# Six weight tiles instead of four in the group behind each norm of the feed-forward stages

## The chip, the cores and the metric

The kernel runs on one core of a Trainium2 chip. The metric is the device time of one execution in microseconds. TensorE (PE) multiplies, PEld is its weight load, VectorE (DVE), ScalarE (ACT) and GpSimd (POOL) work elementwise, SyncE (SP) issues most loads. SBUF is the on-chip memory, PSUM the eight banks that TensorE writes to.

## The reference

Two transformer blocks follow each other on one sequence of 256 tokens and 2048 channels, in float32. Each has mixers and feed-forward stages behind RMS norms. The change touches the three feed-forward stages:

```python
# first block, one stage
f = jnp.square(jax.nn.relu(rms_norm(h, norm_mlp_pre[i]) @ mlp_w1[i])) @ mlp_w2[i]
h = h + rms_norm(f, norm_mlp_post[i])
# second block, two stages (layer 0 and 1)
gate, up = jnp.split(rms_norm_2(h, g[2]) @ w_ffn_in, 2, axis=-1)
h = h + rms_norm_2((jax.nn.silu(gate) * up) @ w_ffn_out, g[3])
```

The first has 8192 hidden channels, the other two 5632 each. The output is h after both blocks.

## The kernel before

**Numbers.** Float32 values are multiplied as two float32r parts, high and low. `split` (L243) makes them of an activation tile, `wload` (L255) of weights: a load into `wr`, the high part `wh` on ScalarE (L263), the low part `wl` on VectorE (L264). The pool has four buffers for each of `wr`, `wh` and `wl`, so the split of a chunk needs the buffer of the chunk four before it.

**A group.** `group` (L289) multiplies several weight tiles of 128 output channels, j, with all 16 tiles x of 128 input channels, k. Each j has a PSUM bank of its own. The weights come in chunks of `kc` = 2 k's and four j's, 1024 columns. For each k and j there are two products (L306): `wh` with both parts of x, 512 columns, and `wl` with the high part, 256 columns. Afterwards `evac` (L365) adds the halves of a bank (ScalarE L382, VectorE L384), and the stage's own operations make the hidden tile H of it.

**The banks.** There are eight: four of the tag "ps", two "px", two "pm" (L193). With `self.alt` set, as it is in the feed-forward stages, a group takes four "ps" banks, or two "px" and two "ps", or two "ps" and two "px" in turn (L301 to L303, counted by `gpar`, which `post_norm` sets so that the first group of a stage takes four "ps"). Small matters and the background work take "pm".

**The first group of a stage** stands right behind the norm before it, and its x does not exist yet. `pre(k)` (L546) makes it: `upd` (L599) adds the normed output to h (VectorE L603), `tile_T` (L585) turns a tile of h by two transposes on TensorE (L591) into half a "px" bank, so two k's share a bank; then ScalarE makes the high part of x (L250) and VectorE the low part (L251). The second transposes of a bank wait until the first half has been read. The norm's factor (L551) is worked out beside that and is multiplied in later.

**The order.** Each engine runs its own queue of instructions in order. The queues are filled ahead of time by a scheduler that takes what is ready by its model, in the order of priorities. Background work for the S5 mixer (`bg_step`) has a lower priority and runs mainly on GpSimd.

**The stages.** `mlp` (L1157) and `ffn` (L1546) go through the hidden channels in four or three parts. A part has groups of four tiles (in `ffn` two tiles of the gate and the same two of the up half), then the product with the second weight (`outs`, L349, `atok`, L334).

Of the kernel before, what the change touches and what calls it, by code (L numbers as in the profile page):

```python
# [18 lines left out]
P = 128  # L19
# [118 lines left out]
class K:  # L138
# [150 lines left out]
    def group(self, Xk, ks, load, ntile=4, pre=None, narrow=None, tag="ps", kc=2):  # L289

        nc = self.nc
        narrow = not self.alt if narrow is None else narrow
        lhs = lambda w, kk, j: w[:, kk, j * P:(j + 1) * P]
        if narrow:
            banks = [self.ps(tag) for _ in range(ntile // 2)]
            ps = [banks[j // 2][:, (j % 2) * T:(j % 2 + 1) * T] for j in range(ntile)]
        else:
            tags = ["ps"] * 4  # L300
            if self.alt:  # L301
                self.gpar = (self.gpar + 1) % 3
                tags = [["ps"] * 4, ["px", "px", "ps", "ps"], ["ps", "ps", "px", "px"]][self.gpar]  # L303
            ps = [self.ps(tags[j]) for j in range(ntile)]
        n = len(ks)
        mm = lambda o, w, x, a, z: nc.tensor.matmul(o, w, x, start=a, stop=z, skip_group_check=True)  # L306
        for c in range(0, n, kc):
            if pre:
                for k in ks[c:c + kc]:
                    pre(k)  # L310
            wh, wl = load(ks[c])

            order = [(kk, j) for j in range(ntile) for kk in range(kc)]
            if pre and c + kc < n:
                order = [(kk, j) for kk in range(kc) for j in range(ntile)]
            if narrow:
                for kk, j in order:
                    i = c + kk  # L320
                    X = Xk(ks[i])
                    mm(ps[j], lhs(wh, kk, j), X[:, 0], i == 0 and j % 2 == 0, False)
                    mm(ps[j], lhs(wh, kk, j), X[:, 1], False, False)
                    mm(ps[j], lhs(wl, kk, j), X[:, 0], False, i == n - 1)
            else:
                for a in range(0, len(order), 2):
                    for kk, j in order[a:a + 2]:
                        mm(ps[j], lhs(wh, kk, j), Xk(ks[c + kk]), c + kk == 0, False)
                    for kk, j in order[a:a + 2]:
                        mm(ps[j][:, 0:T], lhs(wl, kk, j), Xk(ks[c + kk])[:, 0], False, c + kk == n - 1)  # L330
            self.mix_step()
        return ps
# [252 lines left out]
    def tile_T(self, k, bank={}):  # L585

        if k % 2 == 0:
            bank[0] = self.ps("px")
        pt = bank[0][:, (k % 2) * T:(k % 2 + 1) * T]
        for c in range(2):  # L590
            self.nc.tensor.transpose(pt[:, c * P:(c + 1) * P], self.h[:, c, k * P:(k + 1) * P], self.ident)  # L591
        return pt
# [564 lines left out]
    def mlp(self):  # L1157
        nc, I = self.nc, self.I
        V, S = nc.vector, nc.scalar
        X, pre = self.make_x(("mlp_pre", 0))  # L1160
        W1, W2 = I["mlp_w1"], I["mlp_w2"]
        Y = self.newY()
        ss = self.sums()
        ks = list(range(16))
        for ch in range(4):
            H = self.newX()
            self.bg_drain = ch == 3
            for gi in range(4):
                if not pre:
                    self.bg_step(1.5)  # L1170
                c0 = ch * 2048 + gi * 512
                ps = self.group(lambda k: self.xk(X, k), ks, lambda k0: self.wload([((slice(None),), self.wsrc(W1, k0, c0))]),
                                pre=pre)
                if pre:
                    pre = None
                    self.dump("h1", self.h)
                    r2 = self.s([P, 2], tag="r2")
                    rt = self.h_norm()
                    V.tensor_tensor(r2, rt, rt, op=ALU.mult)
                for j in range(4):  # L1180
                    z = self.evac(ps[j])
                    f = self.e()
                    V.scalar_tensor_tensor(f, z, 0.0, z, op0=ALU.max, op1=ALU.mult)
                    behind = self.split(self.xk(H, gi * 4 + j), f)

            def step(gi):
                if ch < 3:
                    self.bg_step(1.5)
                elif gi < 2:
                    self.bg_step(1)  # L1190
                elif gi == 2:
                    self.bg_clean()

            for cols, pv in self.outs(lambda k: self.xk(H, k), ks, W2, ch * 16, ch == 3, step):
                self.add_up(Y, cols, pv, ch, ss if ch == 3 else None, 1)
        self.ple_proj(0, behind)
        self.upd = self.post_norm(Y, ss, r2)
        self.ple_proj(1)
# [347 lines left out]
    def ffn(self, layer):  # L1546
        nc, I = self.nc, self.I
        V, S = nc.vector, nc.scalar
        X, pre = self.make_x(("ng2", layer * 64 + 32))
        rb = self.rtile("a")  # L1550
        W1, W2 = I["w_ffn_in_2"][layer], I["w_ffn_out_2"][layer]
        Y = self.newY()
        ss = self.sums()
        sl = lambda a, b: (slice(None), slice(None), slice(a, b))
        k_lo = 0
        for nk in (16, 16, 12):
            H = self.newX()
            for gi in range(nk // 2):
                if not pre:
                    self.bg_step(2)  # L1560
                c0 = (k_lo + gi * 2) * P
                ps = self.group(lambda k: self.xk(X, k), list(range(16)),
                                lambda k0: self.wload([(sl(0, 256), self.wsrc(W1, k0, c0, 2, 256)),
                                                       (sl(256, 512), self.wsrc(W1, k0, 5632 + c0, 2, 256))]),
                                pre=pre)
                if pre:
                    pre = None
                    self.dump("hm%d" % layer, self.h)
                    rt = self.h_norm(rb, "rf")
                for j in range(2):  # L1570
                    zg = self.evac(ps[j], mul=rb)
                    S.activation(zg, zg, AF.Silu)
                    zu = self.evac(ps[2 + j])
                    f = self.e()
                    V.tensor_tensor(f, zg, zu, op=ALU.mult)  # L1575
                    self.split(self.xk(H, gi * 2 + j), f)
            last = k_lo + nk == 44
            for cols, pv in self.outs(lambda k: self.xk(H, k), list(range(nk)), W2, k_lo, last, lambda gi: self.bg_step(2)):
                self.add_up(Y, cols, pv, k_lo, ss if last else None, 2 + layer * 4 + 3)
            k_lo += nk  # L1580
        self.bg_end()
        self.upd = self.post_norm(Y, ss, rt)
# [491 lines left out]
```

## Time and profile before

| | us |
|---|---|
| median of 3 runs (3555.54 to 3560.48) | 3558.7 |
| the profiled execution | 3564.73 |
| its span | 3563.0 |
| TensorE busy | 3424.4 (96%) |
| VectorE busy | 2186.2 (61%) |
| ScalarE busy | 1729.6 (49%) |
| GpSimd busy | 907.8 (25%) |
| first group, stage one: first transpose at | 432.24 |
| first group, stage two | 1721.64 |
| first group, stage three | 2798.43 |

TensorE is busy nearly always, so the places where it is not are what to look at. A row of a timeline gives the start, the time taken, engine, line and operation, and in brackets how long the engine had been idle and which instruction ended that. Products are pipelined: the time of one row overlaps the start of the next. The profiled execution ran 6.0 us longer than the median of the runs.

### The profile page before, as it was taken

Reading aid. Unit: us, or ns where it says so; the run is one execution under the profiler, and the core shown is the slowest. Engines: PE = TensorE matmul, PEld = TensorE weight load, DVE = VectorE, ACT = ScalarE, POOL = GpSimd, SP = SyncE. Lnnn points to the kernel's source line nnn. Section 1 sums busy time; section 2 is a strip of 40 time slices with the busy share of each in tenths; the row PEclk is TensorE's granted clock in tenths of the full one; section 3 lists DMA queues with packets and bytes.
Section 4 is the critical chain, followed back from the end, with each engine's and each line's share of the span. In section 5 each row is a group of like instructions: output and inputs, shape, how many; then the busy total and the mean of one; then the engine's idle time right before and its main releaser. Section 6 shows DMA issues by size and latency. Waiting matters only on the chain.

```text
span 3563.0 us, 53866 instructions
## 1 busy us (share of the span) xinstructions
PE 3424.4 (96%) x19926; PEld 2922.6 (82%) x19926; DVE 2186.2 (61%) x3331; ACT 1729.6 (49%) x2613; POOL 907.8 (25%) x1374
## 2 busy tenths in 40 slices
PE   8999999999999999999899999999689899999998
PEld 8877788888888788998788888788568788888887
DVE  6687774556555657455765566576755655455555
ACT  5656654644444444446444444344454544444444
POOL 0231022299620003000534754565400000000000
PEclk9999999999999999999999999999889999999999
DMA  8634456667766564565576777778976565665654
GB/s 265 213 117 152 150 171 193 186 219 221 244 207 200 171 182 140 148 188 180 167 215 219 243 227 230 233 233 272 288 240 200 152 189 190 192 189 191 192 188 146
DMA packets 510080, 707.60 MB, mean 199 GB/s; under 512 B 43926, under 2 KB 316087, under 8 KB 509816
## 3 DMA queue, kind: packets, MB, share of 16 engines
q1 hardware_dynamic: 477648, 637.38, 57.3%
q0 software_dynamic: 27456, 63.65, 5.7%
q8 instruction: 156, 2.56, 0.3%
q10 hardware_dynamic: 4712, 3.13, 0.3%
q14 instruction: 108, 0.88, 0.1%
HBM read 662.56 MB, written 37.22 MB: 196 GB/s over the span
## 4 chain that ended last, share of the span: by engine, by line
PE 46%; DVE 2%; DMA 1%; issue 1%; ACT 1%; SPq 0%; ACTq 0%; DVEq 0%
PE ps L306 18%; PE px L306 8%; PE ps L814 6%; PE ps L815 6%; PE ps L816 6%; PE pm L1791 1%; PE px L591 0%; DVE wl L264 0%; DMA wr<-in_w_ffn_in_dram 0%; ACT wh L263 0%; DMA G<-in_gain_dram 0%; PE ps L1911 0%; DMA wr<-in_w_ffn_out_dram 0%; PE pm L1923 0%; PE px L1911 0%
## 5 line engine op out<-in xcount | busy, mean ns | idle before, releaser
L264 DVE TENSOR_TENSOR wl<-wr,wh 128x1024 fp32r<-128x1024 f32 x1126 | 1447.0, 1287 | 1206.8 <-ACT wh L263 1204.2
L263 ACT ACTIVATE wh<-wr 128x1024 fp32r<-128x1024 f32 x1126 | 1190.5, 1059 | 1415.1 <-PE ps L816 571.2
L306 PE MATMUL ps<-x,wh 128*128 128x512 f32 (+1 forms) x4672 | 1224.3, 352 | 33.7 <-DVE x L251 17.0
L814 PE MATMUL ps<-wh,x 128*128 128x512 f32 (+1 forms) x2160 | 819.6, 380 | 2.8 <-ACT x L247 1.6
L815 PE MATMUL ps<-wl,x 128*128 128x512 f32 (+1 forms) x2160 | 813.6, 377 | 1.3 <-DVE wl L264 1.3
L306 PE MATMUL ps<-x,wl 128*128 128x256 f32 x3648 | 813.3, 282 | 1.5 <-DVE wl L264 1.5
L816 PE MATMUL ps<-wh,x 128*128 128x512 f32 (+1 forms) x2160 | 812.7, 377 | 0.0
L306 PEld LDWEIGHTS ps<-x,wl 128*128 128x128 f32 x3648 | 692.9, 191 | 120.8 <-DVE wl L264 3.3
L306 PEld LDWEIGHTS ps<-x,wh 128*128 128x128 f32 x4672 | 731.4, 192 | 50.8 <-DVE x L251 21.8
L814 PEld LDWEIGHTS ps<-wh,x 128*128 128x128 f32 x2160 | 407.5, 189 | 84.1 <-ACT x L247 4.7
L816 PEld LDWEIGHTS ps<-wh,x 128*128 128x128 f32 x2160 | 407.2, 189 | 75.6 <-issue 2.2
L815 PEld LDWEIGHTS ps<-wl,x 128*128 128x128 f32 x2160 | 407.8, 189 | 74.0 <-issue 1.6
L306 PE MATMUL px<-x,wh 128*128 128x512 f32 x1216 | 383.8, 396 | 4.1 <-DVE e L384 4.1
L306 PEld LDWEIGHTS px<-x,wl 128*128 128x128 f32 x1216 | 228.4, 188 | 54.7 <-issue 0.8
L306 PE MATMUL px<-x,wl 128*128 128x256 f32 x1216 | 239.9, 278 | 0.0
L306 PEld LDWEIGHTS px<-x,wh 128*128 128x128 f32 x1216 | 186.4, 189 | 8.0 <-issue 4.5
L1833 POOL TENSOR_TENSOR m<-m,m 128x128 f32<-128x128 f32 x128 | 71.2, 576 | 165.8 <-PE pm L1791 164.4
L247 ACT ACTIVATE x<-e 128x256 fp32r<-128x256 f32 x168 | 67.2, 410 | 85.8 <-DVE e L1575 50.2
L248 DVE TENSOR_TENSOR x<-e,x 128x256 fp32r<-128x256 f32 x168 | 79.2, 482 | 13.7 <-ACT x L247 10.8
L591 PE MATMUL px<-cst,x 128*128 128x128 f32 x224 | 53.4, 339 | 34.2 <-DVE x L603 18.9
L1850 POOL TENSOR_TENSOR m<-m,m 128x256 f32<-128x256 f32 x64 | 61.7, 965 | 80.3 <-DMA m<-in_s5bT_dram 80.2
L1832 POOL TENSOR_TENSOR m<-m,m 128x128 f32<-128x128 f32 x128 | 78.9, 639 | 0.6
(489 smaller groups left out, 2623.0 us busy)
## 6 DMA issues: line engine op xcount, KB each, us to landing
wr<-in_w_ffn_in_dram SPq DMA_DIRECT2D x704, 256.0 KB, 3.1
wr<-in_mlp_w_dram SPq DMA_DIRECT2D x256, 512.0 KB, 4.5
wr<-in_w_ffn_out_dram SPq DMA_DIRECT2D x176, 512.0 KB, 4.8
wr<-in_w_in_dram SPq DMA_DIRECT2D x152, 512.0 KB, 3.9
wr<-in_w_out_dram SPq DMA_DIRECT2D x64, 512.0 KB, 3.8
wr<-in_w_glu_dram SPq DMA_DIRECT2D x128, 256.0 KB, 3.0
wr<-in_ple_gate_dram SPq DMA_DIRECT2D x32, 512.0 KB, 3.9
wr<-in_w_in_dram SPq DMA_DIRECT2D x32, 256.0 KB, 3.2
```

The lines of the kernel that those rows point to most:

```text
L247: a = nc.scalar.activation(dst[:, 0], src, AF.Copy)
L248: b = (eng or nc.vector).tensor_tensor(dst[:, 1], src, dst[:, 0].bitcast(F32), op=ALU.subtract)
L263: nc.scalar.activation(wh, wr, AF.Copy)
L264: nc.vector.tensor_tensor(wl, wr, wh.bitcast(F32), op=ALU.subtract)
L306: mm = lambda o, w, x, a, z: nc.tensor.matmul(o, w, x, start=a, stop=z, skip_group_check=True)
L591: self.nc.tensor.transpose(pt[:, c * P:(c + 1) * P], self.h[:, c, k * P:(k + 1) * P], self.ident)
L814: nc.tensor.matmul(ps, xh, wh, start=first, stop=False, skip_group_check=True)
L815: nc.tensor.matmul(ps, xh, wl, start=False, stop=False, skip_group_check=True)
L816: nc.tensor.matmul(ps, xl, wh, start=False, stop=last, skip_group_check=True)
L1832: G_.tensor_tensor(cx[:, q], u_(0), l_(0), op=ALU.mult)
L1833: G_.tensor_tensor(t1[:, q], u_(1), l_(1), op=ALU.mult)
L1850: G_.tensor_tensor(ob[:, :, ri], v4(gb[0][:, 0]), v4(gb[1][:, ri]), op=ALU.mult)
```

## The change

The first group of each stage gets six tiles, in chunks of one k, 768 columns: in `mlp` six tiles, then 4, 4 and 2; in `ffn` three of the gate and three of the up half, then six groups of two and two, then one and one. The last has chunks of four k's, with rows of 256 columns (1 KB) in `mlp` and 128 (512 bytes) in `ffn`. The six tiles take the four "ps" and both "px" banks, so `tile_T` turns h in "pm" banks wherever `alt` is set. `gpar` no longer moves in the first group, so the group behind it is the one that takes four "ps" banks.

```diff
@@ -297,8 +297,8 @@
-            tags = ["ps"] * 4
-            if self.alt:
+            tags = ["ps"] * 4 + ["px"] * 2
+            if self.alt and ntile < 6:
                 self.gpar = (self.gpar + 1) % 3
@@ -585,7 +585,7 @@
         if k % 2 == 0:
-            bank[0] = self.ps("px")
+            bank[0] = self.ps("pm" if self.alt else "px")
@@ -1165,23 +1165,24 @@
-            for gi in range(4):
+            for t0, nt, kc in ((0, 6, 1), (6, 4, 2), (10, 4, 2), (14, 2, 4)) if pre else [(4 * i, 4, 2) for i in range(4)]:
                 if not pre:
                     self.bg_step(1.5)
-                c0 = ch * 2048 + gi * 512
-                ps = self.group(lambda k: self.xk(X, k), ks, lambda k0: self.wload([((slice(None),), self.wsrc(W1, k0, c0))]),
-                                pre=pre)
+                c0 = ch * 2048 + t0 * P
+                ps = self.group(lambda k: self.xk(X, k), ks, lambda k0: self.wload(
+                    [((slice(None),), self.wsrc(W1, k0, c0, kc, nt * P))], (P, kc, nt * P)), ntile=nt, kc=kc, pre=pre)
...
-                for j in range(4):
+                for j in range(nt):
...
-                    behind = self.split(self.xk(H, gi * 4 + j), f)
+                    behind = self.split(self.xk(H, t0 + j), f)
@@ -1555,25 +1556,28 @@
-            for gi in range(nk // 2):
+            parts = [(2 * i, 2, 2) for i in range(nk // 2)]
+            if pre:
+                parts = [(0, 3, 1)] + [(3 + 2 * i, 2, 2) for i in range(6)] + [(15, 1, 4)]
+            for t0, nt, kc in parts:
                 if not pre:
                     self.bg_step(2)
-                c0 = (k_lo + gi * 2) * P
+                c0, w = (k_lo + t0) * P, nt * P
                 ps = self.group(lambda k: self.xk(X, k), list(range(16)),
-                                lambda k0: self.wload([(sl(0, 256), self.wsrc(W1, k0, c0, 2, 256)),
-                                                       (sl(256, 512), self.wsrc(W1, k0, 5632 + c0, 2, 256))]),
-                                pre=pre)
+                                lambda k0: self.wload([(sl(0, w), self.wsrc(W1, k0, c0, kc, w)),
+                                                       (sl(w, 2 * w), self.wsrc(W1, k0, 5632 + c0, kc, w))], (P, kc, 2 * w)),
+                                ntile=2 * nt, kc=kc, pre=pre)
...
-                for j in range(2):
+                for j in range(nt):
...
-                    zu = self.evac(ps[2 + j])
+                    zu = self.evac(ps[nt + j])
```

**TensorE's queue, first stage, before**, around k 3. `ps_4905` to `ps_4908` are the four tiles, `wh_4955` and `wh_4988` chunks of two k's, `px_4977` the bank of k 4 and k 5, `cst` the identity, `x_4881` h:

```order
L306 MATMUL ps_4908<-x_4899,wl_4956 128x256
L591 MATMUL px_4977<-cst,x_4881 128x128 x2
L306 MATMUL ps_4905<-x_4899,wh_4955 128x512
L306 MATMUL ps_4906<-x_4899,wh_4955 128x512
L306 MATMUL ps_4905<-x_4899,wl_4956 128x256
L306 MATMUL ps_4906<-x_4899,wl_4956 128x256
L306 MATMUL ps_4907<-x_4899,wh_4955 128x512
L306 MATMUL ps_4908<-x_4899,wh_4955 128x512
L306 MATMUL ps_4907<-x_4899,wl_4956 128x256
L306 MATMUL ps_4908<-x_4899,wl_4956 128x256
L591 MATMUL px_4977<-cst,x_4881 128x128 x2
L306 MATMUL ps_4905<-x_4899,wh_4988 128x512
```

The transposes of k 4 stand ahead of the products of k 3, those of k 5 ahead of the products of k 4 (`wh_4988`).

**TensorE's queue, first stage, now**, from the last products of k 3 (`wh_4989`) to the first of k 4 (`wh_5014`). `pm_5007` is the bank of k 4 and k 5, `pm_5054` that of k 6 and k 7:

```order
L306 MATMUL px_4910<-x_4899,wh_4989 128x512
L306 MATMUL px_4909<-x_4899,wl_4990 128x256
L306 MATMUL px_4910<-x_4899,wl_4990 128x256
L591 MATMUL pm_5007<-cst,x_4881 128x128 x2
L591 MATMUL pm_5054<-cst,x_4881 128x128 x2
L306 MATMUL ps_4905<-x_4899,wh_5014 128x512
L306 MATMUL ps_4906<-x_4899,wh_5014 128x512
L306 MATMUL ps_4905<-x_4899,wl_5015 128x256
```

The transposes of k 4 and k 6 now stand behind all products of k 3 and right ahead of those of k 4. Between k 4 and k 5 (`wh_5036`) the queue reads:

```order
L306 MATMUL px_4909<-x_4899,wl_5015 128x256
L306 MATMUL px_4910<-x_4899,wl_5015 128x256
L591 MATMUL pm_5007<-cst,x_4881 128x128 x2
L591 MATMUL pm_5054<-cst,x_4881 128x128 x2
L306 MATMUL ps_4905<-x_4899,wh_5036 128x512
L306 MATMUL ps_4906<-x_4899,wh_5036 128x512
```

The products of k 5, 6 and 7 then follow without transposes, and the pattern returns at k 8 and k 12, in all three stages.

**VectorE's queue, first stage, before.** The low parts of x (L251) come in pairs behind each weight split; `px_5010` is the bank of k 6 and k 7, `px_5043` that of k 8 and k 9:

```order
L264 TENSOR_TENSOR wl_5121<-wr_5118,wh_5120 128x1024
L251 SCALAR_TENSOR_TENSOR x_4899<-px_5010,vec,x_4899 128x256
L251 SCALAR_TENSOR_TENSOR x_4900<-px_5043,vec,x_4900 128x256
L264 TENSOR_TENSOR wl_5154<-wr_5151,wh_5153 128x1024
L251 SCALAR_TENSOR_TENSOR x_4900<-px_5043,vec,x_4900 128x256
L251 SCALAR_TENSOR_TENSOR x_4900<-px_5076,vec,x_4900 128x256
```

**VectorE's queue, first stage, now.** `wl_5084` is the chunk of k 7, `wl_5109` that of k 8:

```order
L264 TENSOR_TENSOR wl_5084<-wr_5081,wh_5083 128x768
L251 SCALAR_TENSOR_TENSOR x_4899<-pm_5007,vec,x_4899 128x256
L251 SCALAR_TENSOR_TENSOR x_4899<-pm_5054,vec,x_4899 128x256
L264 TENSOR_TENSOR wl_5109<-wr_5106,wh_5108 128x768
L251 SCALAR_TENSOR_TENSOR x_4899<-pm_5007,vec,x_4899 128x256
L251 SCALAR_TENSOR_TENSOR x_4899<-pm_5054,vec,x_4899 128x256
L264 TENSOR_TENSOR wl_5131<-wr_5128,wh_5130 128x768
L264 TENSOR_TENSOR wl_5156<-wr_5153,wh_5155 128x768
L264 TENSOR_TENSOR wl_5178<-wr_5175,wh_5177 128x768
L251 SCALAR_TENSOR_TENSOR x_4900<-pm_5101,vec,x_4900 128x256
```

The low part of k 4 stands behind the split of chunk 7, which needs the buffer of chunk 3; that of k 5 behind the split of chunk 8, which needs the buffer of chunk 4. ScalarE's queue has the same order with L263 and L250.

## Rows read from the trace of the kernel before

**Rows 1.** Lines, TensorE, 432–482, 1721–1764, 2798–2832: count | busy, mean ns | idle.

```profile
L306 PE MATMUL ps<-x,wh 128*128 128x512 f32 x84 | 29.2, 429 | 4.7 <-DVE x L251 4.7
...
L306 PE MATMUL ps<-x,wh 128*128 128x512 f32 x60 | 23.4, 479 | 7.6 <-DVE x L251 7.6
...
L306 PE MATMUL ps<-x,wh 128*128 128x512 f32 x60 | 21.0, 434 | 4.4 <-DVE x L251 4.4
```

**Rows 2.** Timeline of TensorE, first stage: start, us, operation, count, idle before it.

```profile
432.24 1.67 PE L591 MATMUL px<-cst,x 128*128 128x128 f32 x4 [4.87 <-DVE x L603]
...
434.56 1.20 PE L306 MATMUL ps<-x,wh 128*128 128x512 f32 x2
...
437.27 0.90 PE L306 MATMUL ps<-x,wh 128*128 128x512 f32 x2
...
459.04 0.73 PE L306 MATMUL ps<-x,wh 128*128 128x512 f32 x2 [0.76 <-DVE x L251]
...
463.32 0.73 PE L306 MATMUL ps<-x,wh 128*128 128x512 f32 x2 [0.76 <-DVE x L251]
```

**Rows 3.** Timeline of ScalarE, first stage; L247 is a pass of 256 columns.

```profile
456.27 1.06 ACT L263 ACTIVATE wh<-wr 128x1024 fp32r<-128x1024 f32 x1 [1.72 <-PE ps L306]
...
460.55 1.06 ACT L263 ACTIVATE wh<-wr 128x1024 fp32r<-128x1024 f32 x1 [1.76 <-PE ps L306]
...
474.78 0.40 ACT L247 ACTIVATE x<-e 128x256 fp32r<-128x256 f32 x1
```

**Rows 4.** Timeline of VectorE, first stage; L248 is a pass of 256 columns.

```profile
433.69 0.48 DVE L251 SCALAR_TENSOR_TENSOR x<-px,vec,x 128x256 fp32r<-128x256 f32 x1
...
457.37 1.22 DVE L264 TENSOR_TENSOR wl<-wr,wh 128x1024 fp32r<-128x1024 f32 x1 [2.27 <-ACT wh L263]
458.51 0.87 DVE L251 SCALAR_TENSOR_TENSOR x<-px,vec,x 128x256 fp32r<-128x256 f32 x2
...
476.05 0.42 DVE L248 TENSOR_TENSOR x<-e,x 128x256 fp32r<-128x256 f32 x1
```

**Rows 5.** Windows: length; busy (PE, PEld, DVE, ACT, POOL); PEclk, DMA, GB/s.

```profile
463.50:500.00 36.50, 36.50 (x208) 31.63 (x209) 29.11 (x73) 20.82 (x33) 0.00 (x0) 1.00 0.59 176
1722.00:1760.00 38.00, 30.18 (x154) 24.87 (x153) 28.49 (x52) 17.76 (x37) 27.07 (x45) 0.83 0.43 137
...
2775.00:2790.00 15.00, 15.00 (x128) 15.00 (x127) 7.11 (x9) 6.92 (x12) 0.00 (x0) 1.00 0.70 201
```

**Rows 6.** The chain that ended last, in order of time: start, us, what.

```profile
1839.62 1.39 PE px L306 x8
```

**Rows 7.** Lines, VectorE, 1731 to 1762 in stage two.

```profile
L264 DVE TENSOR_TENSOR wl<-wr,wh 128x1024 fp32r<-128x1024 f32 x5 | 10.7, 2147 | 6.0 <-ACT wh L263 6.0
L251 DVE SCALAR_TENSOR_TENSOR x<-px,vec,x 128x256 fp32r<-128x256 f32 x12 | 5.3, 474 | 1.4 <-ACT x L250 1.4
```

**Rows 8.** Timeline of TensorE, stage two.

```profile
1721.64 1.61 PE L591 MATMUL px<-cst,x 128*128 128x128 f32 x4 [4.92 <-issue]
...
1737.65 0.73 PE L306 MATMUL ps<-x,wh 128*128 128x512 f32 x2 [2.71 <-DVE x L251]
...
1738.53 1.06 PE L306 MATMUL ps<-x,wh 128*128 128x512 f32 x2
...
1760.09 0.73 PE L306 MATMUL ps<-x,wh 128*128 128x512 f32 x2 [1.27 <-DVE x L251]
...
1790.46 0.73 PE L306 MATMUL px<-x,wh 128*128 128x512 f32 x2 [1.83 <-DVE e L384]
...
1794.44 0.70 PE L306 MATMUL px<-x,wh 128*128 128x512 f32 x2 [1.85 <-DVE e L384]
...
1818.78 0.69 PE L306 MATMUL ps<-x,wh 128*128 128x512 f32 x2 [1.79 <-DVE e L384]
...
1820.66 1.05 PE L306 MATMUL ps<-x,wh 128*128 128x512 f32 x2
```

More of the change, by code (lines that the diff above doesn't have):

```diff
@@ L1569, in ffn @@
                     rt = self.h_norm(rb, "rf")
-                for j in range(2):
+                for j in range(nt):
                     zg = self.evac(ps[j], mul=rb)
                     S.activation(zg, zg, AF.Silu)
-                    zu = self.evac(ps[2 + j])
+                    zu = self.evac(ps[nt + j])
                     f = self.e()
                     V.tensor_tensor(f, zg, zu, op=ALU.mult)
-                    self.split(self.xk(H, gi * 2 + j), f)
+                    self.split(self.xk(H, t0 + j), f)
             last = k_lo + nk == 44
```

## The prediction

> **What bounds the kernel now.** I read the lines view of TensorE first, over the first group of each feed-forward stage: the stretch in which x is made tile by tile (transposes, L591; its high half on ScalarE, L250; its low half on VectorE, L251) while TensorE already multiplies. TensorE sits idle there for 4.7, 7.6 and 4.4 us, all of it ended by L251 [rows 1]: 16.7 us is all that filling this idle time can give. The timelines of the first stage show why it waits [rows 2 to 4]. The weights of a chunk are split four chunks ahead, since the tags wr, wh and wl have four buffers; so the split of wh starts when a chunk's last product is done (ScalarE at 456.27), wl follows at 457.37, and L251 stands behind wl in VectorE's queue (458.51). TensorE goes on at 459.04, 2.77 us after the chunk ended; in that time it has only one other k to do, and 0.76 us stay idle. From 463.32 on nothing is idle: TensorE is busy for 36.50 of 36.50 us [rows 5]. So whatever lengthens this first group lengthens the kernel.
>
> **The sum of what is moved.** TensorE's products stay the same in number. I call one weight tile times one k a step: 4 of them take 1.39 us [rows 6], 0.348 us each. What the diff does not say is where the transposes land, and the order tells it. Before, the transposes of k stand at least one k of products ahead of those that use them. After, they stand four at a time: k 4 and 6 behind the products of k 3, and right ahead of those of k 4; then k 5 and 7 behind the products of k 4. So nothing covers the way from transpose to product, seven times in a stage (k 0 to 1, 3 to 4, 4 to 5, 7 to 8, 8 to 9, 11 to 12, 12 to 13). And L250 and L251 stand behind the split of the chunk four ahead, which waits for the very products that have just ended.
>
> *The price of one such gap.* It is the chain of before, 2.77 us, with 768 columns in place of 1024: on ScalarE 1.06 against 0.40 us for 256 [rows 3], so 0.22 less; on VectorE 1.22 against 0.42 [rows 4], so 0.27 less: 2.28 us. Its bounds: 2.77 if a narrow split is no shorter, 2.19 if it shrinks by the full quarter; I take 2.28, as both slopes are measured. Four transposes run inside it.
>
> *A stage, from the first transpose at 432.24.* The products of k 0 start when its L251 is done (433.69 plus 0.53, the same step as 458.51 to 459.04), at 434.22. Four steps there take 2.71 us (434.56 to 437.27), at the lower clock level, so six take some 4.0: 438.2. A gap: 440.5. k 1 to 3: four steps from first product to the split that waits for them are 1.51 us (459.04 to 460.55), six 2.21, each further k 6 x 0.348 = 2.09, so 6.39: 446.9. Then three times gap, k, gap, three k: 2.28 + 2.21 + 2.28 + 6.39 = 13.16. That ends at 486.4, and 0.5 later since the split in the last gap is 1024 wide again: 486.9. Before, 13 x 4 = 52 steps are done at 463.32; the 44 that make 96 follow without idle time, 15.3 us and 0.3 for transposes: 478.9. The difference is **8.0 us**: the idle 4.7 us goes, and seven uncovered gaps come.
>
> *The end of the group.* The next group now takes the four "ps" banks, where it took two free "px" banks. Its first product needs L384 of the first tile, which stands behind a 1024-wide split that waits for k 14: 1.10 + 1.14 for the split, then 0.42 for a pass of 256 columns [rows 4] and 0.05 to be seen, 2.7 us after k 14, while k 15 covers 2.09. That adds **0.6 us**; between nothing (L384 early enough) and 1.5 (one more wl ahead of it).
>
> *Stages one and three:* 8.6 us each; the third has nearly the same idle time as the first [rows 1]. *Stage two:* GpSimd works in it for 27 of 38 us [rows 5], wl takes 2.15 us in the mean instead of 1.22, L251 stays at 0.47 [rows 7], and from first transpose to the products of k 13 it takes 38.45 us (1721.64 to 1760.09 [rows 8]) against 31.08 in the first: 7.4 more. After, some five of the seven gaps fall under GpSimd's work, each longer by three quarters of 0.92, 3.5 us; and two gaps are so long that the clock falls, as it did before after 2.71 us of idle time, 1.3 us each (four steps 2.71 in place of 1.39 us). That makes 6.1 in place of 7.4, so the stage adds 7.3. GPSIMD Engine Reference of the Trainium skill, section 1, says that GpSimd shares its SBUF interfaces with VectorE and collides with instructions of two SBUF inputs: wl is one, L251, with one input in PSUM, is not, and the trace agrees in the two means. If every VectorE instruction were stretched alike, L251's 0.47 would grow too, some 0.4 us a gap and 2 us in all.
>
> *The clock in stages one and three.* A gap has some 1.7 us of idle time beside 0.6 us of transposes. In the trace, 1.79 us idle ahead of 1818.78 were followed by pairs of 1.05 in place of 0.63 us from 1820.66 on, the level of 1.2 GHz; 1.83 and 1.85 us ahead of 1790.46 and 1794.44 were not [rows 8]. So it is a toss of a coin, from none to most of the seven gaps; I take one stretch a stage, 2 x 1.3 = 2.6 us.
>
> *Edits taken at nothing.* Turning h in "pm" leaves the order in the other stages that use it (the gate after the first stage, the S5 mixer, the end) as it was. Four more splits a stage run on ScalarE and VectorE beside products. The last group has weight rows of 512 bytes; the w_glu stage reads such rows at 201 GB/s with TensorE busy for 15.00 of 15.00 us [rows 5]; if that cover failed, a chunk would wait for the part of a load beyond its 2.8 us of products. In stage two, idle time of 1.83, 1.85 and 1.79 us behind late evacuations [rows 8] may shrink as the group before it gets longer: between 0 and -5.5; I take 0, since loads run only four chunks ahead in both.
>
> Sum: 8.6 + 7.3 + 8.6 + 2.6 = **27 us**. On the profiled execution's own 3564.73 us this is 3591.8; it lies 6.0 above the median of the runs, so against 3558.7 it is **3586 us**.
>
> **Rivals.** *The gaps are shorter* (if x did not stand behind the splits, only transpose, L250 and L251 would be on the way: 0.4 + 0.47 + 0.53, 1.4 us): seven gaps lose 0.9 each, a stage is slower by some 2.3, in all +7: 3566. Against it speaks the order on both engines, and that the same queueing sets the 2.77 us now. *The other side, faster:* the idle time is filled as the six tiles suggest. Place: the products of k 4, 8 and 12; price: -4.7, -7.6 and -4.4, less the 0.6 at each end, 3544. It turns on whether the transposes for the next four k run before TensorE is out of ready work; for it speaks that six tiles are 2.09 us a k against a chain of 2.28, so that one k of lead would hide it; against it, that they stand behind all ready products in TensorE's own queue. *The clock:* each gap, not one a stage, leaves a stretch at 1.2 GHz: some five more in stages one and three, three in stage two, 13 x 1.3 = +17: 3603. TensorE: Matmul & The Clock Gate of the Trainium skill, section "A second HAM failure mode: psum-queue depth-cycling", tells of a kernel in which short idle times between groups of products made the clock swing. In the rows it follows one idle time of that length in three [rows 8].
>
> **How the numbers follow.** Chances: forecast 0.76, with its own range from 3575 (no lower clock in stages one and three, the late evacuations gone) to 3598 (four more stretches, the larger bound of the gap); clock 0.10; shorter gaps 0.08; faster 0.06. The range that leaves no more than 2 in 10 out: 3567 to 3600, since it loses most of the clock rival, the faster one and half of the shorter gaps. A measurement of this kernel tells 0.2%, some 7 us, from no change: faster is the one rival, 0.06; same is most of the shorter gaps, 0.06; slower is the rest, 0.88.
>
> **What would show it.** Right: in the first group of a stage TensorE idle seven times for 1.5 to 2 us, ended by L251, each right behind four transposes (or two pairs), idle time of some 12 us a stage in place of 4.4 to 7.6; from first transpose to the end of k 15 some 54 to 55 us in stages one and three; splits of 768 columns at 0.85 us on ScalarE and 0.96 on VectorE; pairs at the lower clock level here and there. Wrong: products of k 4 that follow those of k 3 without idle time, or transposes that the chip has run earlier than the queue says. The sum is mis-sized if the gap is not 2.28, if the 0.6 at the group's end is several us, or if the granted clock of the stages falls far below 0.9.

## The result, and the profile after

The changed kernel takes 3588.2 us (median of 4 runs, 3580.4 to 3589.2) against 3558.9: 1.008 times as long, 95% interval 1.0066 to 1.0094, which is 23 to 33 us. Run again beside later experiments it took 3585.9 against 3560.0, a ratio of 1.0073 (1.0060 to 1.0087). TensorE does the same work in a longer span, as the head of the page shows (busy us, share of the span, instructions):

```profile
span 3578.6 us, 53976 instructions
PE 3425.3 (96%) x19926; PEld 2923.0 (82%) x19926; DVE 2181.5 (61%) x3343; ACT 1728.2 (48%) x2625; POOL 908.9 (25%) x1374
```

The lines of TensorE over the three norm groups, up to the end of k 15, answer [rows 1] (count | busy, mean ns | idle time and what ended it):

```profile
L306 PE MATMUL ps<-x,wh 128*128 128x512 f32 x64 | 21.8, 424 | 12.4 <-DVE x L251 12.4
...
L306 PE MATMUL ps<-x,wh 128*128 128x512 f32 x64 | 22.8, 439 | 15.7 <-DVE x L251 15.7
...
L306 PE MATMUL ps<-x,wh 128*128 128x512 f32 x64 | 22.8, 440 | 11.9 <-DVE x L251 11.9
```

Idle time ended by L251 was 4.7, 7.6 and 4.4 us; it is now 12.4, 15.7 and 11.9, 23.3 us more. The timeline of TensorE in stage one shows it gap by gap, where [rows 2] stood before:

```profile
430.59 1.61 PE L591 MATMUL pm<-cst,x 128*128 128x128 f32 x4 [4.43 <-issue]
...
444.78 0.40 PE L306 MATMUL px<-x,wl 128*128 128x256 f32 x2
445.02 0.60 PE L591 MATMUL pm<-cst,x 128*128 128x128 f32 x4
447.26 0.72 PE L306 MATMUL ps<-x,wh 128*128 128x512 f32 x2 [1.65 <-DVE x L251]
...
449.46 0.60 PE L591 MATMUL pm<-cst,x 128*128 128x128 f32 x4
451.76 0.73 PE L306 MATMUL ps<-x,wh 128*128 128x512 f32 x2 [1.70 <-DVE x L251]
...
478.51 0.73 PE L306 MATMUL ps<-x,wh 128*128 128x512 f32 x2 [2.13 <-DVE x L251]
...
484.66 0.39 PE L306 MATMUL px<-x,wl 128*128 128x256 f32 x2
485.52 0.72 PE L306 MATMUL ps<-x,wh 128*128 128x512 f32 x2 [0.47 <-DVE e L384]
```

The products of k 3 run into the transposes at 445.02; those of k 4 start at 447.26. Four transposes take 0.60 us of these 2.24; the rest is idle. There are seven such gaps, ahead of k 1, 4, 5, 8, 9, 12 and 13; between them nothing is idle. The first is 2.17 us, the next five 2.24 to 2.30. The last one is longer, 2.73 us, as the split in it is 1024 columns wide. ScalarE and then VectorE inside the gap that begins at 445.02, where [rows 3, 4] stood:

```profile
444.98 0.84 ACT L263 ACTIVATE wh<-wr 128x768 fp32r<-128x768 f32 x1 [1.24 <-PE px L306]
445.73 0.82 ACT L250 ACTIVATE x<-pm,vec 128x256 fp32r<-128x256 f32 x2
```

```profile
445.86 0.96 DVE L264 TENSOR_TENSOR wl<-wr,wh 128x768 fp32r<-128x768 f32 x1 [0.20 <-ACT wh L263]
446.73 0.87 DVE L251 SCALAR_TENSOR_TENSOR x<-pm,vec,x 128x256 fp32r<-128x256 f32 x2
```

The split of chunk 7 starts when the products of k 3 are done (444.98), and L250 and L251 follow it on their engines. The transposes were done at 445.62; x waits for a split that TensorE needs only three k's later.

### The profile page after: what moved, and what is told of

The parts are those of the page before. It is cut to its first block, busy times and chain, and to the rows that moved or that the text cites. A ratio compares the mean times of both kernels' runs of the same rounds, so it can differ in the third digit from the quotient of the medians.

```text
span 3578.6 us, 53976 instructions
## 1 busy us (share of the span) xinstructions
PE 3425.3 (96%) x19926; PEld 2923.0 (82%) x19926; DVE 2181.5 (61%) x3343; ACT 1728.2 (48%) x2625; POOL 908.9 (25%) x1374
## 5 line engine op out<-in xcount | busy, mean ns | idle before, releaser
L264 DVE TENSOR_TENSOR wl<-wr,wh 128x1024 fp32r<-128x1024 f32 (+1 forms) x1138 | 1445.0, 1272 | 1233.5 <-ACT wh L263 1225.6
L263 ACT ACTIVATE wh<-wr 128x1024 fp32r<-128x1024 f32 (+1 forms) x1138 | 1192.9, 1050 | 1468.9 <-PE ps L816 559.8
L306 PE MATMUL ps<-x,wh 128*128 128x512 f32 (+1 forms) x4608 | 1202.5, 350 | 53.6 <-DVE x L251 40.3
L814 PE MATMUL ps<-wh,x 128*128 128x512 f32 (+1 forms) x2160 | 818.4, 379 | 3.1 <-ACT x L247 1.6
L306 PE MATMUL ps<-x,wl 128*128 128x256 f32 x3584 | 801.3, 282 | 1.3 <-DVE wl L264 1.3
L306 PEld LDWEIGHTS ps<-x,wh 128*128 128x128 f32 x4608 | 718.8, 192 | 74.9 <-DVE x L251 46.8
L306 PEld LDWEIGHTS ps<-x,wl 128*128 128x128 f32 x3584 | 680.3, 191 | 118.7 <-issue 4.1
L814 PEld LDWEIGHTS ps<-wh,x 128*128 128x128 f32 x2160 | 407.0, 189 | 82.4 <-ACT x L247 4.7
L306 PE MATMUL px<-x,wh 128*128 128x512 f32 x1280 | 404.8, 398 | 0.0
L306 PEld LDWEIGHTS px<-x,wl 128*128 128x128 f32 x1280 | 242.2, 189 | 57.4
L306 PE MATMUL px<-x,wl 128*128 128x256 f32 x1280 | 252.9, 279 | 0.0
L247 ACT ACTIVATE x<-e 128x256 fp32r<-128x256 f32 x168 | 67.2, 409 | 72.5 <-DVE e L1579 35.5
L248 DVE TENSOR_TENSOR x<-e,x 128x256 fp32r<-128x256 f32 x168 | 78.4, 477 | 12.8 <-ACT x L247 9.5
L568 ACT ACTIVATE m<-x 128x512 f32<-128x512 f32 (+2 forms) x116 | 63.2, 547 | 23.4 <-DVE x L1208 11.5
```

The costliest lines, as they stand in the source:

```text
L247: a = nc.scalar.activation(dst[:, 0], src, AF.Copy)
L248: b = (eng or nc.vector).tensor_tensor(dst[:, 1], src, dst[:, 0].bitcast(F32), op=ALU.subtract)
L263: nc.scalar.activation(wh, wr, AF.Copy)
L264: nc.vector.tensor_tensor(wl, wr, wh.bitcast(F32), op=ALU.subtract)
L568: self.last_act = self.nc.scalar.activation(self.m([P, 512])[:, 0:y.shape[-1]], y, AF.Square, accum_out=ss[0][:, c, ss[1]:ss[1] + 1])
L814: nc.tensor.matmul(ps, xh, wh, start=first, stop=False, skip_group_check=True)
```

## The experiments

Beside medians I compare the **first part** of a stage: from its first transpose to the first product with the second weight (L814), as in these rows of TensorE's timeline in stage two, which belong in turn to the kernel before (its transposes began at 1721.64 [rows 8]), the same kernel in a second trace, and the changed kernel:

```profile
1931.33 0.40 PE L814 MATMUL ps<-wh,x 128*128 128x512 f32 x1
```

```profile
1720.57 1.62 PE L591 MATMUL px<-cst,x 128*128 128x128 f32 x4 [4.92 <-issue]
...
1921.31 0.40 PE L814 MATMUL ps<-wh,x 128*128 128x512 f32 x1
```

```profile
1725.81 0.68 PE L591 MATMUL pm<-cst,x 128*128 128x128 f32 x2 [4.43 <-issue]
...
1937.34 0.40 PE L814 MATMUL ps<-wh,x 128*128 128x512 f32 x1
```

| kernel | first part, us, stage 1 / 2 / 3 | median us | ratio to before (95%) |
|---|---|---|---|
| before, trace of the prediction | 103.0 / 209.7 / 191.6 | 3558.9 | |
| before, again (e8) | 102.5 / 200.7 / 191.5 | 3558.8 | 0.9999 (0.9990 to 1.0008) |
| changed | 111.0 / 211.5 / 201.5 | 3588.2 | 1.0080 (1.0066 to 1.0094) |
| changed, again (e5) | 111.0 / 213.4 / 201.4 | 3585.9 | 1.0073 (1.0060 to 1.0087) |
| pm banks alone (e1) | 102.2 / 200.2 / 190.3 | 3556.5 | 0.9994 (0.9985 to 1.0003) |
| four tiles, one k (e2) | 110.2 / 228.9 / 197.9 | 3591.9 | 1.0099 (1.0085 to 1.0113) |
| four tiles, one k, pm (e7) | 107.5 / 209.9 / 195.6 | 3573.2 | 1.0037 (1.0025 to 1.0049) |
| six tiles, two k's ahead (e3) | 97.6 / 203.5 / 186.7 | 3548.7 | 0.9974 (0.9965 to 0.9983) |
| six tiles, one k ahead (e4) | 98.2 / 205.3 / 186.5 | 3545.8 | 0.9968 (0.9957 to 0.9979) |
| four tiles, four k's ahead, pm (e6) | 96.6 / 197.0 / 186.6 | 3543.6 | 0.9952 (0.9939 to 0.9965) |

Each ratio is to the kernel before in runs beside it, whose medians were 3558.4 us for e1 to e4, 3560.0 for e5 to e7 and 3559.2 for e8.

**Theory:** chunks of one k bring the transposes right ahead of the products that use them, and x queues behind a split that waits for the products just done; so seven gaps a stage. **Rivals:** the six tiles, the banks or the group's end cost the time; the lower clock does.

### e1: the pm banks alone

```diff
-            bank[0] = self.ps("px")
+            bank[0] = self.ps("pm" if self.alt else "px")
```

> The kernel before with one edit: h is turned in pm banks in the feed-forward stages; groups stay at four tiles and chunks of two k's. Theory (the loss comes from the seven uncovered gaps): stages one and three as before, within 1 us each, L251-ended idle of 4.7 and 4.4 us stays. In stage two the background products on pm now stand behind the norm group, so the three late evacuations of 1.83, 1.85 and 1.79 us may go: 3553 to 3559 in all. Rival (the banks cost the time): 3565 or more, with new idle time ahead of transposes.

Measured: no difference (0.9994). The banks cost nothing that shows; stage three's first part is 1.2 us shorter than in e8, a little more than the 1 us expected. Stage two took 200.2 us against 209.7 in the trace of the prediction, without the three late evacuations, which looked like a gain of the banks; e8 shows that it is none.

### e2 and e7: four tiles in chunks of one k

In the kernel before, with `px` banks (e2) and with the edit of e1 as well (e7):

```diff
-                c0 = ch * 2048 + gi * 512
-                ps = self.group(lambda k: self.xk(X, k), ks, lambda k0: self.wload([((slice(None),), self.wsrc(W1, k0, c0))]),
-                                pre=pre)
+                c0, kc = ch * 2048 + gi * 512, 1 if pre else 2
+                ps = self.group(lambda k: self.xk(X, k), ks, lambda k0: self.wload([((slice(None),), self.wsrc(W1, k0, c0, kc))], (P, kc, 512)),
+                                kc=kc, pre=pre)
```

and alike in `ffn`.

> The kernel before with chunks of one k, 512 columns, in the first group of each stage; four tiles and px banks stay. Theory (the chunk of one k takes the transposes' lead away): the same seven gaps, each 1.80 us, since the split ahead of x shrinks with its columns (0.44 us less on ScalarE, 0.53 on VectorE than 2.77); norm group of stage one 39.4 us from first transpose to the end of k 15 against 35.6 before, about +3.8 a stage, 3568 to 3572 with one stretch at the lower clock. If the gap is only transposes, L250 and L251 it is 1.4 and the sum +1 a stage, 3562. If it does not depend on columns it is 2.28 and the sum 3580. Rival (six tiles or the banks cost the time): 3559, no new idle time.

The gaps are there, without six tiles or other banks, and have the forecast size. TensorE, ScalarE and VectorE in e2:

```profile
453.35 0.60 PE L591 MATMUL px<-cst,x 128*128 128x128 f32 x4
455.17 0.73 PE L306 MATMUL ps<-x,wh 128*128 128x512 f32 x2 [1.22 <-DVE x L251]
```

```profile
453.36 0.63 ACT L263 ACTIVATE wh<-wr 128x512 fp32r<-128x512 f32 x1 [0.76 <-PE ps L306]
453.90 0.82 ACT L250 ACTIVATE x<-px,vec 128x256 fp32r<-128x256 f32 x2
```

```profile
454.02 0.69 DVE L264 TENSOR_TENSOR wl<-wr,wh 128x512 fp32r<-128x512 f32 x1 [0.70 <-ACT wh L263]
454.63 0.87 DVE L251 SCALAR_TENSOR_TENSOR x<-px,vec,x 128x256 fp32r<-128x256 f32 x2
```

The gap is 1.82 us (453.35 to 455.17; 1.80 was expected, 1.40 without the queue, 2.28 if columns did not matter). So the split ahead of x sets it: 2.24 us behind 768 columns, 1.82 behind 512. But the sum was 20 us too low. In stage one k 15 ends 43.2 us after the first transpose where 39.4 was expected: the last gap is 2.73 us, as the split in it is 1024 columns wide, and products at the lower clock level stand behind the first gap and the last. Most of the 20 us is one wait in stage two that no theory had:

```profile
1760.17 0.60 PE L591 MATMUL px<-cst,x 128*128 128x128 f32 x4
1777.22 0.64 PE L1791 MATMUL pm<-m,m 128*32 128x128 f32 x2 [16.45 <-POOL m L1834]
```

A product of the background work stands in TensorE's queue ahead of the next k, and GpSimd made its operand late; TensorE was idle for 16.45 us.

> Four tiles in chunks of one k, as before, now with h turned in pm banks, so that the background product of stage two, which kept TensorE waiting for GpSimd for 16.45 us, stands far behind the norm group. Theory: that wait goes, the seven gaps of 1.8 us a stage stay: +7 in stage one, +6 in stage three, about -2 in stage two, 3565 to 3573. If it stays at 3590, the wait was not what made the run with px banks slow.

With the product behind the norm group the wait is gone and the time 18.7 us lower. The first parts are longer than in e8 by 5.0, 9.1 and 4.1 us. The median, 3573.2, lies at the upper end of what was expected: the -2 of stage two rested on the trace of the prediction, and e8 shows that to be no usual one.

### e3 and e4: six tiles, with the lead restored

The changed kernel with `pre` called m k's ahead of the products, m = 2 (e3) or 1 (e4):

```diff
-                for k in ks[c:c + kc]:
+                m = 2 if kc == 1 else 0
+                for k in ks[c + m if c else 0:c + kc + m]:
                     pre(k)
```

> The changed kernel, but the transposes and splits of x are written two k's ahead of the products. Theory: the low part of k stands behind the split that waits for the products of k-3, so two k's of products (4.2 us) cover a chain of 2.28; idle time ended by L251 under 1.5 us in stages one and three, and some 2 us in stage two; 3538 to 3548, faster than before. Rival (banks, the narrow last group or the boundary behind the norm group cost the time): 3560 or more although the gaps are gone.

> As the run with two k's ahead, but one k ahead. Theory: the low part of k stands behind the split that waits for the products of k-2, and one k of products, 2.09 us, covers all but 0.2 us of a chain of 2.28: some 13 idle times of 0.2 us a stage, 2 to 3 us; 3546 to 3556. If the chain were longer than 2.28, every tenth of it would add 1.3 us a stage.

Both are faster than before, by 0.26% and 0.32%, with the banks, the narrow last group and the order at the group's end of the change. e4's rows over the norm groups of stages one and three:

```profile
L591 PE MATMUL pm<-cst,x 128*128 128x128 f32 x32 | 7.5, 314 | 5.1 <-issue 4.4 <-DVE x L251 0.6
...
L591 PE MATMUL pm<-cst,x 128*128 128x128 f32 x32 | 7.5, 316 | 6.1 <-DVE x L603 5.7 <-DVE x L251 0.3
```

L251 ends 0.6 and 0.3 us of idle time where it ended 12.4 and 11.9. The 13 times 0.2 us expected of e4 are not there: between the products of two k's stand two transposes as well, about 0.3 us, and 2.09 and 0.3 cover 2.24. That two k's ahead are not better than one was a miss. e3 lies 0.7 us above its range, e4 just below its own. What is left is in stage two. Of the 2 us of idle time ended by L251 that were expected there in e3 5.0 are left, and in e4 5.6 us ahead of transposes and 3.8 ahead of products:

```profile
L306 PE MATMUL ps<-x,wh 128*128 128x512 f32 x90 | 32.2, 444 | 3.8 <-DVE x L251 3.8
...
L591 PE MATMUL pm<-cst,x 128*128 128x128 f32 x32 | 7.6, 315 | 10.2 <-DVE x L251 5.6 <-issue 4.4 <-DVE x L603 0.2
```

### e6: the lead alone

The kernel before with the edit of e1, four tiles and chunks of two k's, and `pre` four k's ahead:

```diff
-                for k in ks[c:c + kc]:
+                m = 4 if kc == 2 and not narrow else 0
+                for k in ks[c + m if c else 0:c + kc + m]:
                     pre(k)
```

> The kernel before with h turned in pm banks and the transposes and splits of x written four k's ahead; four tiles and chunks of two k's stay. Theory (the lead alone matters, not the number of tiles): L251-ended idle time of 4.7 and 4.4 us in stages one and three goes to under 1, stage two loses most of its 7.6 and the three late evacuations of 5.5: 3540 to 3550, as fast as six tiles with the lead. Rival (six tiles fill the idle time, lead alone doesn't): 3553 to 3559, as the run with pm banks alone.

Measured: 3543.6 us, 16 less than before and the fastest here. Its rows over the three norm groups:

```profile
L306 PE MATMUL ps<-x,wh 128*128 128x512 f32 x88 | 29.8, 417 | 0.0
...
L306 PE MATMUL ps<-x,wh 128*128 128x512 f32 x92 | 32.3, 430 | 0.0
...
L591 PE MATMUL pm<-cst,x 128*128 128x128 f32 x32 | 8.4, 349 | 7.5 <-issue 4.9 <-DVE x L251 2.6
...
L306 PE MATMUL ps<-x,wh 128*128 128x512 f32 x88 | 29.8, 416 | 0.0
```

No product waits for L251 any more, and in stage two transposes still do, for 2.6 us. The idle time that six tiles were to fill is filled by four, once x is made early enough. Against e8 the first parts are shorter by 5.9, 3.7 and 4.9 us, 14.5 in all.

### e5 and e8: both kernels once more

No edit.

> The changed kernel once more, on the chip of the runs beside it, for more executions and a second trace. Theory: the three norm groups again have seven gaps each; the median stays within 3582 to 3590 against 3558. In the first trace the three stages explain +17 us against the trace of before, while the medians differ by 29; if this trace lies near 3588, the stretches that are longer than in the first trace show where the other 8 us are (more stretches at the lower clock level behind gaps, or places outside the three stages).

The seven gaps are there in all three stages, and the three first parts agree with the first trace within 1.9 us. The span is 3584.1 us here, and stage two as a whole, up to the first transpose of stage three, took 6.8 us more than in the first trace, about half of it around one late evacuation, which the first trace does not have:

```profile
2386.55 0.70 PE L306 MATMUL ps<-x,wh 128*128 128x512 f32 x2 [2.07 <-DVE e L384]
```

> The kernel before once more, for a second trace. In the first one (3564.73 us, 6 above the median) the first part of stage two took 209.7 us from the first transpose to the first product with the second weight, with three late evacuations of 1.8 us. The traces of the changed kernel lie 18 and 24 us above it, the medians 26 and 29. Theory: the first trace of before holds some 5 us that a usual execution doesn't, in stage two ahead of 1820 or before the first stage: this one shows 204 to 207 there, or an earlier first transpose, with stages one and three at 103 and 191.6 again. Rival: the same times in all places, and the traces of the changed kernel were both quicker than usual.

Stages one and three repeat within 0.6 us; stage two is 9.0 us shorter, since the three late evacuations of [rows 8] do not occur. TensorE works without a pause in the stretch in which they stood (the columns are those of [rows 5]):

```profile
1773.00:1850.00 77.00, 77.00 (x442) 66.88 (x441) 51.14 (x62) 37.99 (x55) 41.72 (x58) 1.00 0.77 233
```

So the trace on which the prediction rests held an incident of 9 us in stage two that another execution of the same kernel does not have. Against e8 the first parts of the changed kernel are longer by 8.5, 10.8 and 10.0 us, 29.3 in all; the medians differ by 29.2 and, beside e5, 25.9. That 29.3 and 29.2 agree is in part chance: the two traces as a whole differ by 22.8 us (3578.6 and 3555.8), since outside the first parts the changed kernel's is 6.5 us shorter, and it is 7.8 us below the median of its runs. With e5's trace it is 31.1 us in the first parts and 28.3 in all.

## Why the prediction was right

**The forecast** was 3586 us; 3588.2 and 3585.9 were measured, inside its own range of 3575 to 3598.

- *The order.* Seven uncovered gaps a stage, each right behind four transposes, as the queue says. No products of k 4 follow those of k 3 without idle time.
- *The price of a gap*, 2.28 us from 2.77 and the two slopes: measured 2.17 to 2.30 us, and 2.73 for the last (2.78 in the sum). The splits took 0.84 and 0.96 us, as the slopes gave, and the slopes hold at 512 columns as well (e2): 0.63 and 0.69, a gap of 1.82.
- *A stage*, 8.0 us by the end of the norm group: in stage one k 15 ends 54.5 us after the first transpose, 54.7 in the sum. The group's end: 0.47 us idle for L384 (485.52), 0.6 in the sum.
- *Stage two*, 7.3 us: the norm group takes 60.2 us to the end of k 15. Before, by the sum's own reckoning (52 steps until the products of k 13, then 44 of 0.348 and 0.3), it took 54.1 in the first trace and 52.7 in e8, so it adds 6.1 to 7.5, where 6.7 was forecast. The whole first part grew by 10.8 us against e8, more than that. 0.87 us of it is seen: the products of the norm's factor (L424) and two of the background now stand behind k 15 (1786.01 to 1786.88), on a TensorE without idle time, and no longer in the norm group; the other 2.4 us is the background's too. Thirty more of its products stand farther behind, in two stretches that begin with these rows:

```profile
1854.03 0.42 PE L1795 MATMUL pm<-m,m 128*32 128x128 f32 x6
...
1901.30 0.42 PE L1795 MATMUL pm<-m,m 128*32 128x128 f32 x8
```

  Each takes 3.2 us (to 1857.20 and to 1904.48) and holds two steps of the stage's own products, 0.7 us. In e8 there is one such stretch, and the other 16 products stand in the norm group, 12 of them right ahead of an idle time of 2.79 us:

```profile
1745.66 0.63 PE L1791 MATMUL pm<-m,m 128*32 128x128 f32 x12
...
1874.13 0.43 PE L1791 MATMUL pm<-m,m 128*32 128x128 f32 x8
```

  So some 2.5 us of background products moved from a TensorE with idle time to one without. The sum put nothing for that. And one more step was not in it. The longest gap is none of the narrow chain: VectorE first works out the norm's factor and makes `dg` of it (L423), then splits, then makes x:

```profile
1742.97 1.60 DVE L423 TENSOR_SCALAR dg<-cst,rf 128x128 f32<-128x128 f32 x2
1744.50 0.95 DVE L264 TENSOR_TENSOR wl<-wr,wh 128x768 fp32r<-128x768 f32 x1
1745.37 0.87 DVE L251 SCALAR_TENSOR_TENSOR x<-pm,vec,x 128x256 fp32r<-128x256 f32 x2
```

```profile
1745.89 1.22 PE L306 MATMUL ps<-x,wh 128*128 128x512 f32 x2 [5.05 <-DVE x L251]
```

  This gap has 5.05 us of idle time. On the other side, "five gaps longer by 0.69" was too much: three of the seven show 1.65 and 1.70 us as in stage one, and the split beside GpSimd's work was long in one (2.05 us at 1777.13, idle time 2.96). One gap, not two, was followed by the lower clock level; in e5 three were. Within the norm group these errors nearly cancel.
- *The late evacuations* (between 0 and -5.5, taken at 0): taking nothing was right for the medians, for a reason that the prediction did not have; they belong to one execution, not to the kernel.
- *The clock*, 1.3 us in stages one and three each. Stage one: the granted clock is 1.00 through six gaps. Stage three: from its first transpose through the first gap the granted clock is 0.50, the level of 1.2 GHz, and its first part is 10.0 us longer where stage one's is 8.5. In both rows the columns are those of [rows 5]:

```profile
445.00:485.40 40.40, 29.52 (x170) 24.71 (x168) 17.85 (x29) 15.89 (x26) 0.00 (x0) 1.00 0.46 137
...
2804.15:2815.00 10.85, 9.44 (x28) 7.14 (x29) 8.66 (x21) 7.66 (x21) 0.00 (x0) 0.50 0.14 42
```

  No gap brought the clock down here. It was 1.00 until TensorE's pause of 5.67 us ahead of the stage, and 0.50 behind that pause. In e5 it is back at 1.00 ahead of the first gap and falls behind the last one:

```profile
2857.55 0.74 PE L306 MATMUL ps<-x,wh 128*128 128x512 f32 x2 [2.13 <-DVE x L251]
...
2859.26 1.05 PE L306 MATMUL px<-x,wh 128*128 128x512 f32 x2
```

  So it is one stretch in stage three and none in stage one, some 1.5 us (10.0 less 8.5) where 2.6 was taken, and in the first trace not for the reason given. The rival with a stretch behind each gap is wrong.
- *Edits taken at nothing.* The pm banks: e1, nothing. The narrow rows of the last group: e3 and e4 have them and are faster than before.

**Luck.** With the clock's 1.3 us the forecast for the three first parts was 9.9, 7.3 and 9.9 us; against e8 they grew by 8.5, 10.8 and 10.0. Stage one was put 1.4 too high and stage two 3.5 too low, so that the total is nearer than its terms.

**The rivals.** Shorter gaps (1.4 us) are ruled out by the gaps of 2.24 us and by e2; that the idle time gets filled is ruled out by the seven gaps. The condition that the prediction gave for the faster side, one k of lead, was the right one: e4 has just that lead and takes 3545.8, where the rival said 3544.

**What is not settled.** Six tiles with the lead lose 3 to 5 us in the first part of stage two to before, and 6 to 8 to four tiles with the lead. L251 still ends idle time there, and the longest of it stands behind one weight split, which took 3.25 us in e3 and 3.86 in e4, where 0.96 is usual for its shape, while GpSimd is busy. VectorE and then TensorE in e4:

```profile
1740.58 3.86 DVE L264 TENSOR_TENSOR wl<-wr,wh 128x768 fp32r<-128x768 f32 x1 [1.81 <-ACT wh L263]
```

```profile
1744.89 0.44 PE L591 MATMUL pm<-cst,x 128*128 128x128 f32 x2 [2.72 <-DVE x L251]
```

Beside that, e3 has 2.2 us of idle time ended by L384 at the group's end, and both have two stretches of background products behind the norm group where e8 has one. No run has the stage without GpSimd's work, so that this work makes the split long is not shown. Why an execution now and then has late evacuations in stage two is seen twice (e5, the first trace of the kernel before) and explained by no run.

## What to carry to other kernels

Where a chunk's operands are made just ahead of it, the size of a chunk is also the lead of that making: halve the chunk, and what was written a step ahead stands right before its use, on an engine that can't look past it. Read in the queue what stands between a producer and its first reader, and on the producer's engine what stands ahead of it and for what that waits: here a split for a chunk four ahead, in the way of the x that was needed next. Widening the group was the costly way to fill idle times of some 0.8 us each; calling the producer four k's earlier, with its banks moved, took three lines and gave 16 us.

## What the runs showed of the hardware

Idle time of 1.65 to 2.13 us, six times within 40 us, left the granted clock at 1.00 in stage one of the changed kernel. Idle time of that length did not always: 2.13 us in stage one of e2 and in stage three of e5, and 1.77 in stage two of e5, were followed by pairs of 1.05 us, the level of 1.2 GHz. The length of one idle time alone does not tell which will come. TensorE: Matmul & The Clock Gate of the Trainium skill, section "A second HAM failure mode: psum-queue depth-cycling", tells of short idle times between groups of products that make the clock swing; in stage one no swing shows, in the others single falls do.

A matmul of low priority in TensorE's queue stopped it for 16.45 us (e2), since its operand came from GpSimd and was late. Whether such a wait appears depends on a place in the queue that a change of banks moved.

VectorE's weight splits beside GpSimd's work took 1.53 us in the mean in e6, 1.22 in stage one of the same run, where GpSimd rests; L251 took 0.48 in both. GPSIMD Engine Reference of the Trainium skill, section 1, has contention with GpSimd for VectorE instructions with two SBUF inputs, and the two means agree, since L264 has two and L251 takes one of its inputs from PSUM:

```profile
L264 DVE TENSOR_TENSOR wl<-wr,wh 128x1024 fp32r<-128x1024 f32 x11 | 16.9, 1534 | 5.1 <-ACT wh L263 5.1
L251 DVE SCALAR_TENSOR_TENSOR x<-pm,vec,x 128x256 fp32r<-128x256 f32 x15 | 6.9, 478 | 1.5 <-ACT x L250 1.3
```

One profiled execution is one sample. That of the kernel before held 9 us in one stage that its second trace does not have; the other first parts of both kernels differ by at most 1.9 us between two traces.
